# The second block's attention: projection weights split by quarters, one step after each piece of a projection

## The chip, the cores and the metric

The kernel runs on one core of a Trainium2 chip. The metric is device time in microseconds of one execution; the time quoted is the median of three runs. The profile is of one further execution.

## The reference, cut to what matters

Two transformer blocks are computed on 512 tokens of width 1024, in 32-bit floats. The first block mixes (short convolution and FFT), attends to a memory and runs a mixture of experts. The second block, where the change lies, has two kinds of attention heads, read from one projection `w_in_2`, then an output projection and a gated feed-forward part:

```
u = rms_norm(h, norm1_w)
proj = u @ w_in                               # 1024 x 3072
dq, dk, dv, sq, sk, sv = split(proj)
y_diff = two softmaxes per head, subtracted:  (softmax(q0 k0) - lam * softmax(q1 k1)) @ dv
y_sb   = stick-breaking:  sigmoid(z) * product over later keys of sigmoid(-z), @ sv
h = h + concat(rms_norm(y_diff), rms_norm(y_sb)) @ w_out
h = h + (silu(u2 @ w_gate) * (u2 @ w_up)) @ w_down
```

## The kernel before

**Weights.** Every weight matrix is read in chunks of 1024 rows by 256 columns (1 MB, held as 128 partitions by 8 row groups `k` by 256). A product is made with three matmuls in TensorE's rounded 32-bit format: upper part times upper part, upper times lower, lower times upper. So each chunk, once loaded as `raw`, is split into an upper part `wh` (ScalarE copies with rounding, line 241) and a lower part `wl` (VectorE subtracts `wh` from `raw`, line 259).

**The stream.** The chunks stand in a list `stream`, in order of use. `chunk(name)` is called at the head of each projection. It calls `split_to`, which splits the chunk that comes next: there are two buffers for `wh`, so one chunk is in use and one is prepared. `rest` makes the lower part, gives the raw buffer back, and calls `load_to`, which issues the next load from SyncE's queue (line 218). For the chunks of this part of the kernel `wh` is one instruction of 128x2048 and `wl` another. The set `calm` is empty in this kernel.

**The attention part.** The order of the units is `UNITS`: a stick-breaking pair of heads ("s", 0), two pairs of difference heads ("d", 0) and ("d", 1), and ("s", 1). A unit has three chunks, q, k and v, so there are twelve: sq0, sk0, sv0, dq0, dk0, dv0, dq1, dk1, dv1, sq1, sk1, sv1. A projection is made in four pieces, with a call of `tick` after each. In `proj_N` (all v chunks, and dq and dk) a piece is one tile of 128 tokens against all of the chunk, 24 matmuls in order of `k` (from line 274 to line 276); in `proj_T` (sq, sk) the first two pieces use `k` 0 to 3 and the last two `k` 4 to 7. After two pieces of `proj_N` the bank is read out: for v by ScalarE (line 283) and VectorE (line 284), for dq and dk by a sum of squares (lines 1663 to 1668), and a power on GpSimd (line 380).

**The side work.** The heads of a unit run as a `Chain` of steps while later projections are made. `tick` adds the piece's cost to a model time `now`, and runs up to two steps of each of two chains that are due by that model. Letters name the steps: P, Q, R the scores of the query blocks, T the transposes of the weights (line 1495, read out at lines 280 and 281), A the product with v (lines 1507 to 1509), N and C the head norm (1519, 1535). Difference heads have F (line 1717), which finishes the weights of the last block before T. The order of instructions on every engine is the order in which this program writes them down; nothing is reordered by a scheduler.

```
def tick(piece=2.56):
    now[0] += piece
    for g in side[:2]:
        for _ in range(2):
            if g.steps and g.ready():
                g.step()
```

Of the kernel before, what the change touches and what calls it, by code (L numbers as in the profile page):

```python
# [11 lines left out]
F32 = mybir.dt.float32  # L12
F32R = mybir.dt.float32r
# [3 lines left out]
AF = mybir.ActivationFunctionType  # L17
ALU = mybir.AluOpType
# [17 lines left out]
UNITS = (("s", 0), ("d", 0), ("d", 1), ("s", 1))  # L36
# [13 lines left out]
HALVED = 5  # L50
# [35 lines left out]
def block_kernel(ctx: ExitStack, tc: tile.TileContext, a: dict, out: bass.AP, start="mix", stop="tail"):  # L86
    nc = tc.nc
# [12 lines left out]
    def cols(w, c, n=256):  # L100
        return w.rearrange("(k p) f -> p k f", p=P)[:, :, c * n:(c + 1) * n]

    stream = []
# [2 lines left out]
    plan = {}  # L106
    wide = {}
    home = set()
    calm = set()
    pools = {}  # L110

    def add(name, ap, j=None):
        plan[name] = len(stream)
        wide[len(stream)] = j
        stream.append(ap)
# [26 lines left out]
    if "tail" in run:  # L142
        w2 = a["w_in_2"][0]
        for kind, u in UNITS:
            for n, base in zip("qkv", (6, 8, 10) if kind == "s" else (0, 2, 4)):
                add((kind + n, u), cols(w2, base + u))
        for c in range(4):
            if c > 1:
                home.add(len(stream))
            add(("o2", c), cols(a["w_out_2"][0], c))  # L150
        wd = a["w_down_2"][0].rearrange("(k p) f -> p k f", p=P)
        for part, fs in enumerate(FF):
            for c in fs:
                add(("fg", c), cols(a["w_gate_2"][0], c))
                add(("fu", c), cols(a["w_up_2"][0], c))
            k0, k1 = 2 * fs[0], 2 * fs[-1] + 2
            for half in range(2):
                for c, k in enumerate(range(k0, k1, 4)):
                    add(("fd", part, half, c), wd[:, k:min(k + 4, k1), half * 512:half * 512 + 512])

    raws, parts, lows = {}, {}, {}

    room = list(ROOM[0])
    state = {"load": 0, "split": 0, "use": 0, "held": None, "later": None, "last": None,
             "limit": plan[0, "gu", 0] + EARLY if "moe" in run else len(stream)}

    def buffer(b, shape, dt, name):
        pool = rawp if b in ROOM[0] else pools["raw" if b in ROOM[1] else "raw3"]
        return pool.tile(shape, dt, tag=f"w{b}", name=name)

    def hl_pool(i):
        if i in home:
            return "slots"
        return "hl" if wide[i] is not None and wide[i] % 4 >= 2 else None

    def oldest():

        return max(state["use"] - 1, 0) if state["held"] is None else state["held"]

    def pieces(r, two):  # L180
        n = r.shape[1] // 2 if two else r.shape[1]
        return [slice(q, q + n) for q in range(0, r.shape[1], n)]
# [4 lines left out]
    def find(i, low):  # L187


        for q in [q for q in lows if q < oldest()]:  # L190
            room.append(lows.pop(q))
        expert, running = wide[i] is not None, "hl" in pools
        may = room if expert else always(room)
        if low:
            if state["last"] in may:
                may = [state["last"]]
        else:
            if running and len(room) < 2 and len(lows) < 4:
                return None
            if expert and not running:  # L200
                may = [b for b in may if (b in ROOM[0]) == (wide[i] < 2)]
            if not (expert and running) and len(always(room)) < 2 and len(always(lows.values())) < 2:
                may = [b for b in may if b not in ROOM[0]]
        if not may:
            return None
        b = may[0]
        room.remove(b)
        return b

    def load_to(n, queue=nc.sync):  # L210
        while state["load"] < min(n, state["limit"], len(stream)):
            i = state["load"]
            b = find(i, False)
            if b is None:
                return
            r = buffer(b, list(stream[i].shape), F32, "raw")
            for t in pieces(r, i < HALVED):
                queue.dma_start(r[:, t], stream[i][:, t])
            raws[i] = b, r
            state["load"] += 1  # L220

    def split_to(n):
        while state["split"] < min(n, len(stream)):
            i = state["split"]
            key = hl_pool(i)
            busy = sum(hl_pool(q) == key for q in range(oldest(), i))
            if key and key not in pools or busy == 2:
                return
            if key == "slots" and state["use"] + 2 <= i:
                return  # L230
            load_to(i + 1)
            if state["later"] is None and i not in home:
                b = find(i, True)
                if b is None:
                    return
                lows[i] = b
            pool = pools[key] if key else hlp
            b, r = raws.pop(i)
            h = pool.tile(list(r.shape), F32R, tag="s" if key == "slots" else "hi", name="wh")
            for t in pieces(r, i < HALVED):  # L240
                nc.scalar.activation(h[:, t], r[:, t], AF.Copy)  # L241
            parts[i] = h, None
            state["split"] += 1
            if state["later"] is None:
                rest(i, b, r, h)
            else:
                state["later"].append((i, b, r, h))

    def rest(i, b, r, h):
        if i in home:  # L250
            l = pools["slots"].tile(list(r.shape), F32R, tag="s", name="wl")
        else:
            if i not in lows:
                lows[i] = find(i, True)
            l = buffer(lows[i], list(r.shape), F32R, "wl")
        parts[i] = h, l
        engine = nc.gpsimd if i in calm else nc.vector
        for t in pieces(r, i < HALVED or i in calm):
            engine.tensor_tensor(l[:, t], r[:, t], h[:, t].bitcast(F32), ALU.subtract)  # L259
        room.append(b)  # L260
        state["last"] = b
        load_to(len(stream))

    def chunk(name):
        i = plan[name]
        assert i == state["use"], (name, i, state)
        state["use"] += 1
        split_to(i + 4)
        return parts.pop(i)
# [237 lines left out]
    def mixing():  # L507
# [200 lines left out]
        for ct in range(4):  # L708
# [18 lines left out]
            out_half(ps0, ct, 0, *first)  # L727
        state["held"] = None
        split_to(state["use"] + 3)

        hT = []
# [217 lines left out]
    def moe():  # L949
# [20 lines left out]
        later = state["later"] = []  # L970
        state["held"] = state["use"]
        split_to(state["use"] + 4)
        state["held"] = state["later"] = None
        rest(*later.pop(0))

        wide_ = rp.tile([P, NT, NE + K], F32, name="logit")
# [88 lines left out]
        for args in later[:2]:  # L1065
            rest(*args)
# [323 lines left out]
    def tail():  # L1390
# [47 lines left out]
        class Chain:  # L1438
# [12 lines left out]
            def step(self):  # L1451
                name, work, cost, _ = self.steps.pop(0)
                work()
                now[0] += cost
                self.at[name] = now[0]
# [6 lines that stand above are left out]
                        g.step()  # L1462
                if not g.steps:
                    side.remove(g)

        def drain():
            while side:
                g = side[0]
                g.step()
                if not g.steps:  # L1470
                    side.pop(0)

        def parts2(name, late=None):

            r = proj_T(name, hT, late=late, tick=tick)
            return r, slot([P, 2, 2, S])
# [380 lines left out]
        for part, fs in enumerate(FF):  # L1857
            actT = []
            slots_ = []
            for c in fs:  # L1860
                g = []
                for ps in proj_T(("fg", c), h2T, late=(lambda: rsd.visit_to(4)) if c == 0 else None):
                    if rb is None:
                        rb = spread(rsd.rstd(EPS_2), NT, sc, "rbc")
                    t = sc.tile([P, S], F32, tag="om", name="fg", bufs=3)
# [4 lines left out]
                for j, ps in enumerate(proj_T(("fu", c), h2T)):  # L1870
# [3 lines left out]
                    q = len(actT) % 4  # L1874
# [3 lines left out]
            for half in range(2):  # L1878
                s = slice(half * 512, half * 512 + 512)
                ps = [bank() for _ in range(NT)]  # L1880
                for c in range((nf + 3) // 4):
                    h, l = chunk(("fd", part, half, c))
                    n = min(4, nf - 4 * c)
                    for i in range(NT):
                        t = slice(i * P, (i + 1) * P)
# [37 lines left out]
    if "tail" in run:  # L1923
        if "mix" not in run:
            with tc.tile_pool(name="tc", bufs=1) as tp:
                for _ in tail_constants(lambda shape: tp.tile(shape, F32, name="c%d" % len(shape) + str(shape[-1]))):
                    pass
        tail()
    else:
        dump()  # L1930
# [24 lines left out]
```

## Time and profile before

| | us |
|---|---|
| median of three runs | 2212.07 |
| lowest and highest run | 2211.58, 2212.27 |
| the profiled execution, its own time | 2213.85 |
| span of the profiled execution, first to last instruction | 2212.1 |

The profile's page gives busy time by engine, and TensorE's granted clock as a share of 2.4 GHz (0.50 is 1.2 GHz). The twelve attention projections and their side work run from about 1550 to 1764 us of the span; the rest of the second block follows. Times of rows below are us from the span's start.

### The profile page before, as it was taken

The numbers are of one execution on the slowest core, as the hardware profiler recorded it, in microseconds if no ns is written. First come the engines' busy times: TensorE is split into PE (matmuls) and PEld (weight loads), VectorE is DVE, ScalarE is ACT, GpSimd is POOL, SyncE is SP. The second block draws the span as 40 slices with busy tenths as digits, with TensorE's granted clock in tenths as the row PEclk, the third lists the DMA queues.
The fourth block names the chain that finished last, engine by engine and source line by source line (L and its number), as shares of the span: only waits on it lengthen the run. The fifth ranks groups of instructions, "written<-read, shape, count | busy, mean of one in ns | idle before, by whom it ended". The sixth has DMA issues, their size and how long they took to land. (4 is left out here: it accounts for less than half of the span.)

```text
span 2212.1 us, 28473 instructions
## 1 busy us (share of the span) xinstructions
PE 2155.5 (97%) x11282; PEld 1821.3 (82%) x11282; DVE 1594.7 (72%) x1630; ACT 1286.2 (58%) x1365; POOL 372.2 (17%) x237
## 2 busy tenths in 40 slices
PE   8999997999999999999999999998999889999999
PEld 7889897888888888888888888887888788888887
DVE  6555556999999999989898999987676754333342
ACT  5234445777777777777777777774654544221221
POOL 1220015212121212121212112110321000100110
PEclk9999998999999999999999999999999999999999
DMA  6422236999999999999999999997122112322222
GB/s 210 135 66 96 78 114 226 363 376 358 365 346 373 355 373 358 364 360 366 363 363 368 365 364 366 370 352 248 51 64 68 58 58 72 100 95 95 96 86 86
DMA packets 162095, 518.17 MB, mean 234 GB/s; under 512 B 14040, under 2 KB 82531, under 8 KB 129126
## 3 DMA queue, kind: packets, MB, share of 16 engines
q1 hardware_dynamic: 148886, 488.06, 59.7%
q0 software_dynamic: 13056, 28.24, 4.8%
q8 instruction: 90, 1.47, 0.3%
q14 instruction: 47, 0.39, 0.1%
q10 hardware_dynamic: 16, 0.00, 0.0%
HBM read 510.28 MB, written 22.13 MB: 241 GB/s over the span
## 5 line engine op out<-in xcount | busy, mean ns | idle before, releaser
L259 DVE TENSOR_TENSOR wl<-raw,wh 128x2048 fp32r<-128x2048 f32 (+1 forms) x468 | 1046.0, 2263 | 242.9 <-ACT wh L241 241.2
L241 ACT ACTIVATE wh<-raw 128x2048 fp32r<-128x2048 f32 (+1 forms) x468 | 870.8, 1892 | 219.1 <-PE b L1165 70.9
L1164 PE MATMUL b<-wh,xh 128*128 128x512 f32 x1024 | 412.2, 403 | 0.0
L1165 PE MATMUL b<-wh,xl 128*128 128x512 f32 x1024 | 401.8, 392 | 0.0
L274 PE MATMUL b<-wh,s 128*128 128x256 f32 (+2 forms) x904 | 281.3, 311 | 2.5 <-ACT s L280 2.5
L276 PE MATMUL b<-wh,s 128*128 128x256 f32 (+2 forms) x904 | 277.4, 307 | 1.0 <-DVE s L284 0.8
L1170 PE MATMUL b<-wl,xh 128*128 128x512 f32 x1024 | 277.6, 392 | 0.0
L275 PE MATMUL b<-wl,s 128*128 128x256 f32 (+2 forms) x904 | 277.1, 307 | 0.3 <-DVE wl L259 0.3
L1170 PEld LDWEIGHTS b<-wl,xh 128*128 128x128 f32 x1024 | 192.2, 188 | 43.6
L1164 PEld LDWEIGHTS b<-wh,xh 128*128 128x128 f32 x1024 | 192.9, 188 | 41.9 <-ACT xh L280 0.3
L1165 PEld LDWEIGHTS b<-wh,xl 128*128 128x128 f32 x1024 | 193.1, 189 | 39.5 <-DVE xl L281 0.4
L1212 PE MATMUL b<-wh,ah 128*128 128x512 f32 x508 | 200.3, 394 | 0.7 <-ACT ah L280 0.7
L1213 PE MATMUL b<-wh,al 128*128 128x512 f32 x508 | 199.4, 393 | 1.4 <-DVE al L281 1.4
L274 PEld LDWEIGHTS b<-wh,s 128*128 128x128 f32 x904 | 175.0, 194 | 11.6 <-ACT s L280 3.0
L276 PEld LDWEIGHTS b<-wh,s 128*128 128x128 f32 x904 | 174.8, 193 | 8.5 <-DVE s L284 1.0
L275 PEld LDWEIGHTS b<-wl,s 128*128 128x128 f32 x904 | 175.1, 194 | 7.3 <-DVE wl L259 0.5
L1278 POOL DMA_INDIRECT acc<-y,res x30 | 57.4, 1914 | 688.4 <-ACT y L1277 688.4
L1216 PE MATMUL b<-wl,ah 128*128 128x512 f32 x508 | 159.0, 394 | 0.0
L415 PE MATMUL b<-s,wh 128*128 128x512 f32 (+1 forms) x348 | 134.1, 388 | 1.5 <-ACT wh L241 1.5
L416 PE MATMUL b<-s,wh 128*128 128x512 f32 (+1 forms) x348 | 132.9, 384 | 0.0
L274 PE MATMUL b<-s,wh 128*128 128x512 f32 (+1 forms) x324 | 123.9, 383 | 1.0 <-ACT s L283 1.0
L275 PE MATMUL b<-s,wh 128*128 128x512 f32 (+1 forms) x324 | 123.5, 381 | 0.8 <-DVE s L284 0.8
(377 smaller groups left out, 2874.5 us busy)
## 6 DMA issues: line engine op xcount, KB each, us to landing
raw<-in_w_gate_up_dram SPq DMA_DIRECT2D x254, 1024.0 KB
raw<-in_w_down_dram SPq DMA_DIRECT2D x138, 1024.0 KB
raw<-in_w_in_dram SPq DMA_DIRECT2D x19, 1024.0 KB
raw<-in_w_gate_dram SPq DMA_DIRECT2D x11, 1024.0 KB
raw<-in_w_up_dram SPq DMA_DIRECT2D x11, 1024.0 KB
raw<-in_w_out_dram SPq DMA_DIRECT2D x8, 1024.0 KB
raw<-in_w_k_dram SPq DMA_DIRECT2D x8, 512.0 KB
raw<-in_w_q_dram SPq DMA_DIRECT2D x4, 1024.0 KB
```

Source lines behind the costliest of these rows:

```text
L241: nc.scalar.activation(h[:, t], r[:, t], AF.Copy)
L259: engine.tensor_tensor(l[:, t], r[:, t], h[:, t].bitcast(F32), ALU.subtract)
L274: nc.tensor.matmul(ps, ah, bh, start=(first and j == 0), stop=False)
L275: nc.tensor.matmul(ps, ah, bl, start=False, stop=False)
L276: nc.tensor.matmul(ps, al, bh, start=False, stop=(last and j == n - 1))
L415: nc.tensor.matmul(r[j][:, :n], ah, bh, start=q == 0, stop=False)
L1164: nc.tensor.matmul(ps[q], xh[:, k, :], wh[:, q, :], start=(k == 0), stop=False)
L1165: nc.tensor.matmul(ps[q], xl[:, k, :], wh[:, q, :], start=False, stop=False)
L1170: nc.tensor.matmul(ps[q], xh[:, k, :], wl[:, q, :], start=False, stop=(k == ND - 1))
L1212: nc.tensor.matmul(ps[s], ah[:, q, :], wh[:, kk, c], start=(q == 0), stop=False)
L1213: nc.tensor.matmul(ps[s], al[:, q, :], wh[:, kk, c], start=False, stop=False)
L1216: nc.tensor.matmul(ps[s], ah[:, q, :], wl[:, kk, c], start=False, stop=(q == ND - 1))
```

## The change

Nine of the twelve chunks, those of the units ("d", 0), ("d", 1) and ("s", 1), are put into `calm`. `split_to` no longer splits such a chunk at once. It hands it to a new function `drip`, which lays five steps into a list `waiting`. Steps 0 to 3 make one quarter of the upper part each (two row groups `k`, 128x512, ScalarE); steps 1 to 4 make one quarter of the lower part each, one quarter behind (VectorE). Step 4 also gives the raw buffer back and issues the next load. `tick` ends with one step out of `waiting`, behind the side work that it ran. `split_to` begins by running whatever is still waiting, so the fifth step stands at the head of the next projection, the one that uses this chunk. The old use of `calm` (halves on GpSimd), which no chunk had, is taken out.

```
+            if (kind, u) != UNITS[0]:
+                calm.add(len(stream))
             add((kind + n, u), cols(w2, base + u))
...
+    def dripped(n=0):
+        while len(waiting) > n:
+            waiting.pop(0)()
+
+    def drip(i, b, r, h):
+        low = []
+        def lower(t):
+            if not low:
+                low.append(buffer(lows[i], list(r.shape), F32R, "wl"))
+                parts[i] = h, low[0]
+            nc.vector.tensor_tensor(low[0][:, t], r[:, t], h[:, t].bitcast(F32), ALU.subtract)
+
+        def step(q):
+            m = r.shape[1] // 4
+            if q < 4:
+                t = slice(q * m, q * m + m)
+                nc.scalar.activation(h[:, t], r[:, t], AF.Copy)
+            if q > 0:
+                lower(slice(q * m - m, q * m))
+            if q == 4:
+                room.append(b)
+                state["last"] = b
+                load_to(len(stream))
+
+        waiting.extend(lambda q=q: step(q) for q in range(5))
+
     def split_to(n):
+        dripped()
         while state["split"] < min(n, len(stream)):
...
             h = pool.tile(list(r.shape), F32R, tag="s" if key == "slots" else "hi", name="wh")
+            if i in calm:
+                state["split"] += 1
+                drip(i, b, r, h)
+                continue
...
-        engine = nc.gpsimd if i in calm else nc.vector
-        for t in pieces(r, i < HALVED or i in calm):
-            engine.tensor_tensor(l[:, t], r[:, t], h[:, t].bitcast(F32), ALU.subtract)
+        for t in pieces(r, i < HALVED):
+            nc.vector.tensor_tensor(l[:, t], r[:, t], h[:, t].bitcast(F32), ALU.subtract)
...
                 if not g.steps:
                     side.remove(g)
+            dripped(max(len(waiting) - 1, 0))
```

## Rows read from the trace of the kernel before

**Rows 1.** The timeline of PE: start, length; in brackets the idle time and its releaser.

```profile
1624.70 0.87 PE L1686 MATMUL b<-ident,gn 128*128 128x128 f32 x6 [0.67 <-DVE gn L1676]
...
1664.07 1.75 PE L1495 MATMUL b<-ident,e 128*128 128x128 f32 x7 [7.52 <-DVE e L1717]
...
1733.51 0.50 PE L1507 MATMUL b<-ath,s 128*128 128x512 f32 x1 [1.98 <-DVE atl L281]
...
1766.38 0.65 PE L1535 MATMUL b<-ident,hr 128*128 128x128 f32 x4 [2.61 <-POOL hr L380]
```

**Rows 2.** Line 259 on DVE, 1570 to 1775: who on PE waited for it (us, times).

```profile
  PE b L275: 0.3, 1
```

**Rows 3.** The timelines of ACT and DVE: copy and subtraction of 128x512.

```profile
1578.55 0.63 ACT L1564 ACTIVATE s<-t 128x512 fp32r<-128x512 f32 x1 [1.36 <-DVE t L1563]
...
1579.21 0.69 DVE L1565 TENSOR_TENSOR s<-t,s 128x512 fp32r<-128x512 f32 x1 [0.70 <-ACT s L1564]
```

**Rows 4.** The timeline of PE: first matmul of dq0, dk0 (and its 24th), dv0, dq1, dk1, dv1.

```profile
1590.31 0.36 PE L274 MATMUL b<-wh,s 128*128 128x256 f32 x1
...
1607.11 0.36 PE L274 MATMUL b<-wh,s 128*128 128x256 f32 x1
...
1609.95 0.28 PE L276 MATMUL b<-wh,s 128*128 128x256 f32 x1
...
1625.33 0.36 PE L274 MATMUL b<-wh,s 128*128 128x256 f32 x1
...
1648.67 0.39 PE L274 MATMUL b<-wh,s 128*128 128x256 f32 x1
...
1677.55 0.36 PE L274 MATMUL b<-wh,s 128*128 128x256 f32 x1
...
1694.89 0.36 PE L274 MATMUL b<-wh,s 128*128 128x256 f32 x1
```

**Rows 5.** The timeline of DVE: last instructions written down ahead of each projection's head.

```profile
1597.51 0.48 DVE L284 SCALAR_TENSOR_TENSOR s<-b,rr,s 128x256 fp32r<-128x256 f32 x1 [0.55 <-ACT s L283]
...
1610.78 0.23 DVE L1668 TENSOR_SCALAR gr<-gr,rr 128x4 f32<-128x4 f32 x1
...
1629.04 1.40 DVE L284 SCALAR_TENSOR_TENSOR s<-b,gq,s 128x512 fp32r<-128x512 f32 x2
...
1656.77 0.48 DVE L284 SCALAR_TENSOR_TENSOR s<-b,rr,s 128x256 fp32r<-128x256 f32 x1 [0.54 <-ACT s L283]
1658.57 2.29 DVE L259 TENSOR_TENSOR wl<-raw,wh 128x2048 fp32r<-128x2048 f32 x1 [1.31 <-ACT wh L241]
...
1663.27 0.75 DVE L1717 SCALAR_TENSOR_TENSOR e<-e,dr 128x512 f32<-128x512 f32 x1
...
1679.81 0.23 DVE L1668 TENSOR_SCALAR gr<-gr,rr 128x4 f32<-128x4 f32 x1
...
1695.90 1.40 DVE L284 SCALAR_TENSOR_TENSOR s<-b,gq,s 128x512 fp32r<-128x512 f32 x2
```

**Rows 6.** The timelines of PE and ACT at the start: first chunk, split by halves.

```profile
10.61 0.58 PE L415 MATMUL b<-s,wh 128*128 128x256 f32 x1 [1.51 <-ACT wh L241]
...
9.51 1.05 ACT L241 ACTIVATE wh<-raw 128x1024 fp32r<-128x1024 f32 x1
```

**Rows 7.** Windows: stretch, its length, busy time (instructions) by engine, granted clock, DMA.

```profile
1590.30:1593.30 3.00, 3.00 (x27) 3.00 (x28) 2.79 (x5) 3.00 (x7) 0.00 (x0) 1.00 0.00 0
...
1602.00:1606.00 4.00, 4.00 (x32) 3.87 (x31) 3.76 (x12) 2.22 (x7) 1.67 (x1) 1.00 0.81 262
...
1664.00:1666.00 2.00, 1.93 (x9) 1.60 (x11) 1.53 (x12) 1.25 (x5) 0.00 (x0) 0.50 0.67 227
...
1734.00:1736.00 2.00, 2.00 (x9) 1.81 (x8) 1.86 (x9) 0.00 (x0) 0.00 (x0) 0.50 1.02 328
1736.00:1738.00 2.00, 2.00 (x12) 1.42 (x11) 1.13 (x6) 0.80 (x3) 0.00 (x0) 0.64 0.60 198
```

**Rows 8.** The timeline of DVE: a wait for PE between the splits.

```profile
1643.60 0.29 DVE L1746 CUSTOM_DVE_ANT_0 e<-b,bias 128x128 f32<-128x128 f32 x1 [2.15 <-PE b L276]
```

More of the change, by code (lines that the diff above doesn't have):

```diff
@@ L108, in block_kernel @@
     home = set()
-    calm = set()
+    calm, waiting = set(), []
     pools = {}
```

## The prediction, made before the changed kernel ran

> **What bounds the kernel now.** I read the page first, then the timeline of PE through the twelve attention projections, for its idle time, then those of ScalarE and VectorE around each projection's head. PE has work nearly all the time; what can be won is what its idle rows hold [rows 1]. The long one, 7.52 us at 1664.07, is T of unit ("d", 0) waiting for F, and in front of F on VectorE stands a split: the lower part of dk1 runs 1658.57 to 1660.86, F ends at 1664.02 [rows 5]. The 1.98 us at 1733.51 (A of the same kind, one unit later) are of the same sort. The 2.61 us at 1766.38 come from GpSimd's power, behind VectorE's work; the first chunk of the output projection, whose split stands before it, is not among the nine. On the other side, the split as it is hardly ever holds PE up: 0.3 us in all of this stretch [rows 2], because a chunk is ready one whole projection before its use. That lead is what the change spends.
>
> **The change part by part.** *Price of the pieces.* The whole lower part takes 2.29 us [rows 5]. A quarter is 128x512; the nearest rows of that form take 0.69 us on VectorE and 0.63 us on ScalarE [rows 3]. Four cost 2.76 us where one cost 2.29, so 0.5 us more per chunk, and a little more on ScalarE. Between neighbours on the same queue I take 0.6 us per lower quarter and 0.5 per upper one, since such instructions overlap a little. In busy time this is about 10 us over nine chunks on engines with gaps; it costs nothing by itself. The cost is in the order.
>
> *When the last quarter is there.* The step behind piece 4 of a projection writes upper quarter 4 and lower quarter 3 of the next chunk; lower quarter 4 is written down at the head of that chunk's own projection. Both stand on VectorE's queue behind everything that the earlier pieces left there: side work, and the reading out of the last bank. In `proj_N` a piece's 24 matmuls follow each other at 0.1235 us (1607.11 to 1609.95 for 23 steps, [rows 4]) in order of `k`, so the first piece needs lower quarter 4 at its 20th matmul, 2.35 us after its first. That a matmul waits only for the part it reads, and not for the whole tile, is seen at the start of the kernel: the first chunk is split by halves, the first upper half ends at 10.56 and PE starts at 10.61 [rows 6]. So PE stands still at a head if VectorE is later than PE's first matmul there by more than 2.35 us, less the added quarters. I go through the heads; "ends" are of the last VectorE instruction written down ahead of the head.
>
> dq0: PE starts at 1590.31 and needs quarter 4 at 1592.66 [rows 4]. VectorE ends at 1597.99 [rows 5], and is busy 2.79 of 3 us with the score scans while PE makes that piece [rows 7], so three added quarters lie on its way, 1.8 us, and the fourth after them: 1600.45. PE loses **7.8**.
>
> dk0: PE needs it at 1609.46 [rows 4]. VectorE ended at 1611.0 [rows 5], with a split ahead of the step T that now is gone, but T's read-out is then paced by PE and ScalarE; behind it come quarter 3 (0.6) and quarter 4 (0.6): 1612.25. PE loses **2.8**.
>
> dv0: VectorE ended at 1630.4 [rows 5], with waits for GpSimd in which two quarters hide. The first one delays the scaling before PE's transposes (PE already waited there, [rows 1]), so PE starts 0.6 later; quarter 4 is there at 1631.5, needed at 1625.33 + 0.6 + 2.35 = 1628.3. PE loses 0.6 + 3.2 = **3.8**.
>
> dq1: VectorE ends at 1657.25 [rows 5]; one quarter ahead of a head norm (0.6), upper quarter 4 ahead of ScalarE's read-out (0.5) and the last (0.6) give 1659.0, and PE needs it at 1651.0 [rows 4]: 8 us. But this is the stretch of the 7.52 us. PE now waits at the head, and F is done when PE comes to T (head's last matmuls 0.7, a norm and the scores 1.5, piece two 3.0, T's first transposes 0.4: 1664.6 against 1664.07). So the long wait is only moved, at **+0.5**; two small waits ahead of it, whose split is gone, give back **-0.6**.
>
> dk1: VectorE ends at 1680.0 [rows 5]; about 1.6 us of quarters and ScalarE's copies do not hide, and quarter 4 follows: 1682.3 against 1679.9. PE loses 2.4, less 0.5 that T waits there today: **1.9**.
>
> dv1: VectorE ends at 1697.3 [rows 5], with the added 1.2 us at 1698.5; needed at 1697.24. PE loses **1.3**.
>
> sq1 and sk1 start with 16 matmuls on the upper part of `k` 0 to 3 alone and need quarter 4 only in piece three: nothing. At sk1 the split goes from in front of A's weights, which takes 0.6 off the 1.98 us and the slow clock behind it; at sv1 the head loses some 3 us. Up to the 2.61 us at 1766.38 [rows 1], which VectorE and GpSimd pace, the two together come to **-0.2**.
>
> The sum of waits is 7.8 + 2.8 + 3.8 + 0.5 - 0.6 + 1.9 + 1.3 - 0.2 = 17.3 us. Losses at early heads are not made good later: VectorE itself waits for PE in between, 2.15 us at 1643.60 [rows 8], so PE's delay goes through to it.
>
> *The clock.* After the 7.52 us the granted clock is 0.50, the lower level of 1.2 GHz, and after the 1.98 us it is 0.50 in 1734 to 1736 and 0.64 in 1736 to 1738 [rows 7]: 1.0 + 0.7 = 1.7 us lost behind that one. I put 1.7 behind the long waits of dq0 and dv0, half of it behind dk0, dk1 and dv1, whose waits come in two parts of 1 to 1.5 us, nothing at dq1, which pays already; 6.0, of which about 1 falls into the waits themselves. That is 5 us.
>
> *Transfers.* Each next load is issued one projection later, when quarter 4 is done. The windows show a load of 1 MB in 1602 to 1606 at 262 GB/s [rows 7], so about 4 us, and its chunk is first touched after the next projection's first piece, at least 12 us later. It stays hidden behind that projection; without that cover each of nine would cost up to 4 us. SyncE's and GpSimd's queues get nothing else new. ScalarE's upper quarters are done before VectorE comes to them.
>
> *Sum.* 17.3 + 5 = 22.3 us on the profiled execution's 2213.85 gives 2236.1; that execution is 1.8 us above the median of the runs, so **2234** for the median, about 1.0% slower.
>
> *Bounds.* From below: added quarters cost nothing ahead of the last, no clock is lost, and sk1's wait goes fully (1.98 + 0.5 + 1.7) with sv1's head free: 6.0 + 0.1 + 3.4 - 1.1 + 0.5 + 0.7 - 4.2 = 5.4 us, 2217. From above: no quarter hides, each head a further 1 to 2 us, sv1's 2.5 us stay, and 1.7 us of clock at five heads: 28 + 8 = 36 us, 2248. Single prices between the ends go by the row that is nearest: full price where VectorE has no idle row, nothing where it waits for GpSimd or PE.
>
> **Rivals.** *Faster: the side work gets through.* Without upper and lower part ahead of it, F's chain starts at 1657.25 and not at 1660.86 [rows 5], so T waits 3.7 us less, and some 0.9 of slow clock goes; A's wait and its slow clock go (1.98 + 1.7), with 0.5 at the next T: 8.8 us, 2203. It decides if quarter 4 of dq0 is there by 1592.66. For it speak the two idle rows; against it the ends in [rows 5], all later than the need in [rows 4] even without one added quarter. The Trainium skill states the rule for it ("Perfetto Trace Analysis", section "Optimizing Scalar/DVE Operations"): where ScalarE and VectorE are not saturated but leave bubbles on other engines, breaking up instructions may let work finish sooner. By that rule alone the time would be 2203; the trace bears it out at T and A, not at the heads.
>
> *No change: PE's delay eats its later idle time.* If VectorE's chain to F at 1663 did not depend on PE, the early heads would only use up the 7.52 us, and the time would be about 2213. Against it: the wait at 1643.60 [rows 8].
>
> *Slower still: a matmul waits for the whole tile.* Then each head loses what it now overlaps, some 2 us in six places and more at sk1, 12 to 18 us on top: 2246 to 2252. Against it: [rows 6].
>
> **How the numbers follow.** The forecast has 0.80, faster 0.10, no change 0.06, the whole tile 0.04. About 0.2%, 4.4 us, is what a measurement of this kernel can tell from no change. Faster by more: 0.10. Within: 0.06 and the forecast's lowest edge, 0.07. Slower: 0.83. The range is the forecast's own bounds, 2217 to 2248; outside lie faster, no change and part of the last.
>
> **What would show it.** In the changed profile PE's longest waits should stand at line 275 or 274 in the first piece of dq0, dk0, dv0 and dq1, released by VectorE's `wl`, in sum over 20 us; T's 7.52 us should be gone from line 1495, with as much at dq1's head; the granted clock should fall to 0.50 behind dq0's head, where it is 1.00 now. If those waits are under 3 us in sum, the reading of VectorE's lag is wrong, and the first rival holds. If PE's lateness at 1764 is much under that at dv0's head, the second does. SyncE's loads should land long before their split.

## The result, and the profile after

The changed kernel takes 2240.4 us (median of four runs, 2236.69 to 2241.41) against 2212.12 for the kernel before (four runs; the 2212.07 above is of three): a ratio of 1.0122, with a 95% interval from 1.0109 to 1.0135. The execution profiled below took 2240.26 us, 26.4 more than the 2213.85 of the one before.

Lines have moved: 274, 275 and 276 of before are now 310, 311 and 312; the transposes T (1495) are 1532, F (1717) is 1754, A (1507) is 1544, and the head norm (1535) is 1572. The reading out of a bank (283, 284) is 319 and 320. New are 244, which makes a quarter of `wh`, and 238, a quarter of `wl`. In some of the experiments the lines stand one or two further down.

From the page of the changed kernel: span, busy time by engine, and the group of line 311.

```profile
span 2238.4 us, 28512 instructions
...
PE 2168.2 (97%) x11282; PEld 1830.9 (82%) x11282; DVE 1595.9 (71%) x1657; ACT 1289.2 (58%) x1392; POOL 368.9 (16%) x237
...
L311 PE MATMUL b<-wl,s 128*128 128x256 f32 (+2 forms) x904 | 282.4, 312 | 23.4 <-DVE wl L238 23.0
```

The last line holds the result in short: PE stood still for 23.0 us at this line because a quarter of `wl` was not yet there. On line 275 of before it was 0.3 [rows 2].

Where the time went is read in two steps. First, how long the stretch from sv0's first matmul to one fixed matmul of the output projection takes (windows, before and then after; the columns are those of [rows 7]):

```profile
1574.92:1840.04 265.12, 243.22 (x1829) 224.00 (x1828) 173.36 (x364) 138.96 (x293) 40.28 (x25) 0.95 0.20 64
```

```profile
1573.90:1866.40 292.50, 257.75 (x1829) 235.16 (x1828) 175.20 (x391) 142.12 (x320) 36.97 (x25) 0.91 0.19 58
```

27.4 us have been added here, so all of the loss lies in this stretch. The matmuls are the same, yet PE is busy 14.5 us longer (257.75 - 243.22), at a granted clock of 0.91 in the mean and not 0.95; it stands idle 12.9 us longer (34.75 against 21.90). VectorE and ScalarE, with 27 more instructions each, are busy only 1.8 and 3.2 us longer. The forecast's 10 us of busy time for smaller pieces came to 5.0, on engines with gaps; the loss is not there.

Second, the heads, that is, the starts of the projections. The first matmul of dq0, dk0, dv0, dq1, dk1 and dv1 in the timeline of PE after; each answers to a row of [rows 4]:

```profile
1589.32 0.36 PE L310 MATMUL b<-wh,s 128*128 128x256 f32 x1
...
1615.73 0.37 PE L310 MATMUL b<-wh,s 128*128 128x256 f32 x1
...
1640.37 0.36 PE L310 MATMUL b<-wh,s 128*128 128x256 f32 x1
...
1667.98 0.39 PE L310 MATMUL b<-wh,s 128*128 128x256 f32 x1
...
1696.59 0.36 PE L310 MATMUL b<-wh,s 128*128 128x256 f32 x1
...
1718.61 0.36 PE L310 MATMUL b<-wh,s 128*128 128x256 f32 x1
```

Minus the starts of before, PE is "late" by -1.0, +8.6, +15.0, +19.3, +19.0 and +23.7 us. (This execution entered the stretch 1.0 us early, so that dq0's -1.0 is zero.) What a head costs is the step to the next one: dq0 9.6, dk0 6.4, dv0 4.3, dq1 -0.3, dk1 4.7; dv1 1.4 more, and sq1, sk1 and sv1 together 1.3. The sum is 27.4.

PE's idle rows at the quarters, in the same timeline (those of dk1 and dv1, 0.40 to 1.14 us, left out), and one row ahead of dv0:

```profile
1592.96 0.39 PE L311 MATMUL b<-wl,s 128*128 128x256 f32 x1 [2.56 <-DVE wl L238]
...
1597.41 0.58 PE L311 MATMUL b<-wl,s 128*128 128x256 f32 x1 [3.01 <-DVE wl L238]
...
1599.43 0.58 PE L311 MATMUL b<-wl,s 128*128 128x256 f32 x1 [0.37 <-DVE wl L238]
...
1618.83 0.39 PE L311 MATMUL b<-wl,s 128*128 128x256 f32 x1 [1.29 <-DVE wl L238]
...
1621.01 0.58 PE L311 MATMUL b<-wl,s 128*128 128x256 f32 x1 [1.20 <-DVE wl L238]
...
1639.74 0.87 PE L1723 MATMUL b<-ident,gn 128*128 128x128 f32 x6 [1.27 <-DVE gn L1713]
...
1646.44 0.39 PE L311 MATMUL b<-wl,s 128*128 128x256 f32 x1 [3.41 <-DVE wl L238]
...
1674.21 0.58 PE L311 MATMUL b<-wl,s 128*128 128x256 f32 x1 [3.63 <-DVE wl L238]
...
1678.33 0.58 PE L311 MATMUL b<-wl,s 128*128 128x256 f32 x1 [2.06 <-DVE wl L238]
...
1774.33 0.58 PE L311 MATMUL b<-wl,s 128*128 128x256 f32 x1 [2.84 <-DVE wl L238]
```

The rows of line 311 stand in the first pieces of dq0, dk0, dv0, dq1 and, the last one, sv1; the row of 1723 is the transposes ahead of dv0. No row of T with 7.52 us is left, nor of A with 1.98 [rows 1]. The second column, the matmul's length, tells of the clock: 0.39 us at 1618.83, but 0.58 at 1621.01, where the granted clock is falling (windows under e9).

What stood in front of dq0's last quarter is seen in VectorE's timeline:

```profile
1592.22 0.68 DVE L238 TENSOR_TENSOR wl<-raw,wh 128x512 fp32r<-128x512 f32 x1
1592.82 1.22 DVE L1640 TENSOR_TENSOR_SCAN om<-om 128x512 f32<-128x512 f32 x1
1594.14 0.69 DVE L1641 TENSOR_TENSOR be<-be,om 128x511 f32<-128x511 f32 x1
1594.75 1.22 DVE L1640 TENSOR_TENSOR_SCAN om<-om 128x512 f32<-128x512 f32 x1
1596.07 0.69 DVE L1641 TENSOR_TENSOR be<-be,om 128x511 f32<-128x511 f32 x1
1596.68 0.68 DVE L238 TENSOR_TENSOR wl<-raw,wh 128x512 fp32r<-128x512 f32 x1
1597.28 0.48 DVE L320 SCALAR_TENSOR_TENSOR s<-b,rr,s 128x256 fp32r<-128x256 f32 x1
1598.30 0.48 DVE L320 SCALAR_TENSOR_TENSOR s<-b,rr,s 128x256 fp32r<-128x256 f32 x1 [0.54 <-ACT s L319]
1598.70 1.28 DVE L238 TENSOR_TENSOR wl<-raw,wh 128x512 fp32r<-128x512 f32 x2
```

The rows of line 238 at 1592.22 and 1596.68 and the first at 1598.70 are quarters two, three and four of dq0; they end where PE's three waits end. The second instruction at 1598.70 is the next chunk's. Between them stand the score scans of the side work (1640, 1641) and the reading out of the last bank (320). VectorE is never idle, except 0.54 us for ScalarE: the quarter is late because of its place in the queue. A quarter begins 0.60 us ahead of its neighbour (1596.68 to 1597.28), the price that the prediction took.

Windows of after behind that head show the slow clock, and the load that the fifth step issues (the last three columns are the granted clock, the DMA share and GB/s):

```profile
1600.00:1602.00 2.00, 2.00 (x12) 2.00 (x11) 0.00 (x0) 0.00 (x0) 0.00 (x0) 0.50 0.55 115
1602.00:1604.00 2.00, 2.00 (x13) 2.00 (x13) 0.00 (x0) 0.00 (x0) 0.00 (x0) 0.63 1.08 379
```

The load comes right behind the last quarter and is mostly over by 1604, 12 us ahead of dk0's first matmul. PE works through these 4 us without idle time, but loses 2 x (0.50 + 0.37) = 1.7 us of them to the clock, where it was at 1.00 before.

### The profile page after: what moved, and what is told of

It is laid out like the page before. It is cut to its first block, busy times and chain, and to the rows that moved or that the text cites. A ratio compares the mean times of both kernels' runs of the same rounds, so it can differ in the third digit from the quotient of the medians.

```text
span 2238.4 us, 28512 instructions
## 1 busy us (share of the span) xinstructions
PE 2168.2 (97%) x11282; PEld 1830.9 (82%) x11282; DVE 1595.9 (71%) x1657; ACT 1289.2 (58%) x1392; POOL 368.9 (16%) x237
## 5 line engine op out<-in xcount | busy, mean ns | idle before, releaser
L295 DVE TENSOR_TENSOR wl<-raw,wh 128x2048 fp32r<-128x2048 f32 (+1 forms) x459 | 1025.3, 2262 | 235.0 <-ACT wh L278 233.3
L278 ACT ACTIVATE wh<-raw 128x2048 fp32r<-128x2048 f32 (+1 forms) x459 | 853.4, 1891 | 218.3 <-PE b L1201 71.0
L311 PE MATMUL b<-wl,s 128*128 128x256 f32 (+2 forms) x904 | 282.4, 312 | 23.4 <-DVE wl L238 23.0
L310 PE MATMUL b<-wh,s 128*128 128x256 f32 (+2 forms) x904 | 284.5, 315 | 3.4 <-ACT s L316 2.6
L312 PE MATMUL b<-wh,s 128*128 128x256 f32 (+2 forms) x904 | 280.7, 311 | 1.0 <-DVE s L320 0.8
L310 PEld LDWEIGHTS b<-wh,s 128*128 128x128 f32 x904 | 178.0, 197 | 13.2 <-ACT s L316 3.1
L312 PEld LDWEIGHTS b<-wh,s 128*128 128x128 f32 x904 | 178.2, 197 | 8.4 <-DVE s L320 1.0
```

The lines of the kernel that those rows point to most:

```text
L295: nc.vector.tensor_tensor(l[:, t], r[:, t], h[:, t].bitcast(F32), ALU.subtract)
L310: nc.tensor.matmul(ps, ah, bh, start=(first and j == 0), stop=False)
L311: nc.tensor.matmul(ps, ah, bl, start=False, stop=False)
L312: nc.tensor.matmul(ps, al, bh, start=False, stop=(last and j == n - 1))
```

## The experiments

Each edit is against the changed kernel; "the stretch" is the one of the two windows above, and all medians are of runs beside the kernel before (2213.03, 2213.66, 2213.78 and 2213.15 in the four groups: e1 to e4, e5 to e8, e9 to e11, e12).

**e1: the five steps at once, at the head.** The pieces stay small, but stand where the whole split stood before.

```
                 drip(i, b, r, h)
+                dripped()
                 continue
```

> The same nine chunks and the same quarters, but all five steps of a chunk are written down at once at the head of the projection before, where the whole split stood. Theory (the last lower quarter stands too far back in VectorE's queue and PE waits for it at the head of its projection): the lead of one projection is back, so the waits at the heads go, the 7.52 us before T and the 1.98 us before A are back, and the time is that of the kernel before within 4 us, 2210 to 2216 us. Rival (the 27 added instructions on each of two engines cost it, wherever they stand): most of the 28 us stays, above 2230 us.

2211.89 us, ratio 0.9993 [0.9983, 1.0003]. The number of instructions costs nothing; the place does. In its profile the stretch is even 2.5 us shorter, though the interval of the ratio reaches 1. The row of T:

```profile
1664.19 1.76 PE L1533 MATMUL b<-ident,e 128*128 128x128 f32 x7 [6.45 <-DVE e L1755]
```

**e8: the same, with the next load issued one projection later,** as in the changed kernel.

```
-            if q > 0:
+            if 0 < q < 5:
                 lower(slice(q * m - m, q * m))
-            if q == 4:
+            if q == 5:
...
-        waiting.extend(lambda q=q: step(q) for q in range(5))
+        for q in range(5):
+            step(q)
+        waiting.append(lambda: step(5))
...
-            dripped(max(len(waiting) - 1, 0))
```

> The nine splits by quarters all at once at the head of the projection before, as in the run that did so, but the raw buffer goes back and the next load is issued one projection later, as in the changed kernel. Theory: the loads of 1 MB take about 4 us and still have more than 10 us, so nothing changes against that run: 2209 to 2215 us. Rival (the later loads are part of the loss): 2217 us or more.

2210.22, ratio 0.9986 [0.9977, 0.9995], and the lateness from head to head of e1 within 0.1 us. Later loads cost nothing.

**e3: only dq0's chunk in steps.**

```
-                if (kind, u) != UNITS[0]:
+                if (kind + n, u) == ("dq", 0):
```

> Only dq0's split is laid out by single steps as in the changed kernel; the other eight chunks are split whole as before. Theory (VectorE and ScalarE wait for PE between dq0's head and T, so PE's delay is not made good): what dq0's head loses, 9.9 us in the changed kernel's trace, comes through to the end, 2219 to 2224 us. Rival (the 7.52 us before T take it up): 2212 to 2216 us.

2221.47, ratio 1.0039 [1.0025, 1.0053]. Its head and its T:

```profile
1593.01 0.38 PE L311 MATMUL b<-wl,s 128*128 128x256 f32 x1 [2.57 <-DVE wl L238]
...
1597.47 0.58 PE L311 MATMUL b<-wl,s 128*128 128x256 f32 x1 [3.49 <-DVE wl L238]
...
1671.75 1.76 PE L1532 MATMUL b<-ident,e 128*128 128x128 f32 x7 [7.52 <-DVE e L1754]
```

8.6 us are lost at the head, and PE stays late by that much at the heads and at the end of the stretch, to within 0.2 us. T still waits 7.52, at 1671.75 and not at 1664.07: an early delay of PE does not use up a later wait.

**e7: only dq1's chunk in steps,** the head next to the 7.52 us (edit as in e3, with `("dq", 1)`).

> Only dq1's split is laid out by single steps; the other eight chunks are split whole as before, dk1's ahead of F among them. Theory: the 8 us that PE loses at dq1's head are the same 7.5 us that it lost before T, since both wait for the same work of VectorE; with dk1's split still ahead of F a wait before T stays as well: 2212 to 2217 us. Rival (the two waits add up): 2219 us or more.

2213.79, ratio 1.0004 [0.9995, 1.0013].

```profile
1650.02 0.39 PE L310 MATMUL b<-wh,s 128*128 128x256 f32 x1 [0.41 <-ACT wh L244]
1654.03 0.58 PE L311 MATMUL b<-wl,s 128*128 128x256 f32 x1 [3.63 <-DVE wl L238]
...
1658.16 0.58 PE L311 MATMUL b<-wl,s 128*128 128x256 f32 x1 [2.06 <-DVE wl L238]
```

6.1 us of waits at the head; T's long wait, of which a part was expected to stay, is gone, and PE comes to dk1 0.5 us earlier than before and to sq1 0.5 us later. The wait moved and was not added to.

**e9: only dk0's chunk in steps** (`("dk", 0)`).

> Only dk0's split is laid out by single steps; the other eight chunks are split whole. In the changed kernel's trace dk0's head is late by 2.6 us and then loses 2.8 us more to the slow clock, where the forecast had 2.8 and 0.85. Theory (a wait in two parts of 1.3 us costs as much slow clock as a long one): 2.5 to 3 us of lateness and 2 to 3 of clock come through to the end, 5 us more than the kernel before. Rival (the slow clock at dk0 was left over from dq0's waits in front of it): 3.5 us more, and the granted clock stays at 1.00 behind dk0's head.

2218.15, ratio 1.0019 [1.001, 1.0028]. Its two waits and a window behind them:

```profile
1608.67 0.39 PE L311 MATMUL b<-wl,s 128*128 128x256 f32 x1 [1.30 <-DVE wl L238]
...
1610.86 0.39 PE L311 MATMUL b<-wl,s 128*128 128x256 f32 x1 [1.21 <-DVE wl L238]
```

```profile
1612.00:1614.00 2.00, 2.00 (x16) 1.62 (x13) 1.76 (x2) 1.36 (x3) 0.30 (x1) 1.00 0.91 270
```

The head costs 3.0 us (2.5 of idle time, 0.5 of busy time), with the granted clock at 1.00 in every window around it. That is the profiled execution, which at 2215.39 us is the second fastest of eleven; they go up to 2220.10, and the median lies 4.4 us above the kernel before, between the theory's 5 and the rival's 3.5. So the 1.00 is shown for one execution. In the changed kernel the same two waits (1.29 and 1.20) were followed by this:

```profile
1620.00:1622.00 2.00, 0.99 (x4) 0.99 (x5) 0.95 (x3) 0.00 (x0) 1.56 (x1) 0.63 0.00 0
1622.00:1624.00 2.00, 2.00 (x12) 1.34 (x11) 0.00 (x0) 0.04 (x1) 0.45 (x1) 0.50 0.94 264
1624.00:1626.00 2.00, 2.00 (x7) 1.71 (x7) 1.32 (x2) 1.95 (x4) 0.00 (x0) 0.50 0.77 261
1626.00:1628.00 2.00, 2.00 (x13) 2.00 (x12) 1.62 (x3) 0.44 (x1) 0.00 (x0) 0.66 0.00 0
```

Against 1.00 PE's busy time in these four windows loses 0.99 x 0.37 + 2.00 x (0.50 + 0.50 + 0.34) = 3.0 us. With the 0.6 us more that the transposes ahead of dv0 wait (1.27 against 0.67), that is about the difference between 6.4 and 3.0. Windows from dk0's first matmul to dv0's, before and then after, give PE's busy time as 3.3 us longer:

```profile
1607.11:1625.33 18.22, 17.55 (x144) 16.27 (x142) 14.43 (x24) 10.56 (x20) 5.25 (x2) 1.00 0.18 58
```

```profile
1615.73:1640.37 24.64, 20.87 (x143) 18.74 (x142) 13.46 (x24) 11.45 (x24) 3.64 (x2) 0.86 0.14 43
```

**e12: dq0 and dk0 in steps,** to see whether the loss at dq0 makes the clock fall at dk0 (`in (("dq", 0), ("dk", 0))`).

> Only the chunks of dq0 and dk0 are split in steps; all else is as before. Alone, dq0 carried 7.7 us to the end and dk0 3.1, and at dk0 alone the granted clock stayed at 1.00 behind waits of 1.30 and 1.21. In the changed kernel, waits of 1.29 and 1.20 at the same place were followed by 0.50 and a cost of 6.4 at that head. Theory: the slow clock at dk0 in the changed kernel comes of what was lost before it on the same way (the long waits and the slow clock at dq0's head, 20 us earlier); then both waits stand here with a granted clock of 0.50 or 0.63 behind them, dk0 costs about 6, and the stretch is 14 us longer: some 0.6% over the kernel before, 2226 to 2229. Rival: the two heads are independent and the clock's answer to such waits is near an edge that differs by execution or by what is done at the following pieces; then the windows behind dk0's head stay at 1.00, dk0 costs 3, and the sum is 10 to 11 us: 2223 to 2225.

2226.46, ratio 1.0058 [1.0044, 1.0072]. The waits at dk0 in its timeline, and the window behind them:

```profile
1619.86 0.39 PE L311 MATMUL b<-wl,s 128*128 128x256 f32 x1 [1.30 <-DVE wl L238]
...
1622.04 0.39 PE L311 MATMUL b<-wl,s 128*128 128x256 f32 x1 [1.21 <-DVE wl L238]
```

```profile
1622.00:1624.00 2.00, 1.96 (x15) 1.54 (x16) 2.00 (x1) 0.18 (x1) 1.48 (x1) 1.00 0.33 65
```

The clock stays at 1.00 from 1616 to 1630, and dk0 costs 3.0 again, dq0 8.6: the losses add up to 11.6, as the rival said. The median came 1.5 us above the rival's band, at the lower edge of the theory's; the windows decide against the theory.

The same trace shows more at dq0. Up to dk0's head e12 has the same instructions as the changed kernel on PE, VectorE, ScalarE and GpSimd, and its first wait at dq0, 2.57 us, is the 2.56 there to within 0.01. Behind it stand, in the changed kernel and then in e12:

```profile
1593.56 0.42 PE L311 MATMUL b<-wl,s 128*128 128x256 f32 x1
```

```profile
1595.05 0.38 PE L311 MATMUL b<-wl,s 128*128 128x256 f32 x1 [2.57 <-DVE wl L238]
...
1595.51 0.28 PE L311 MATMUL b<-wl,s 128*128 128x256 f32 x1
```

The third matmul behind the one that waited takes 0.42 us in one and 0.28 in the other: the clock had fallen in one execution and not yet in the other. dq0 cost 9.6 us in the first and 8.6 in the second.

**e6: the fifth step with the fourth,** behind piece four, so that the last quarter stands ahead of the bank's reading out.

```
             dripped(max(len(waiting) - 1, 0))
+            if len(waiting) == 1:
+                dripped()
```

> As the changed kernel, but the fifth step runs right behind the fourth, after the fourth piece, and so ahead of the reading out of that piece's bank. Theory: VectorE's queue is the cause, and the read-out is a part of what stands in it: quarter 4 comes 1.5 to 3 us earlier at dq0, dk0, dv0, dk1, dv1 and sv1, and T comes 1.5 us earlier; 10 to 12 us less than the changed kernel, 2226 to 2232 us. Rival (only the side work ahead of it holds quarter 4 up): within 3 us of the changed kernel.

2226.94, ratio 1.0059 [1.0044, 1.0075]. About half of the loss goes: the waits at the heads of dv0, dv1 and sv1 are gone, dk0 keeps one of its two (1.29). The other half, above all dq0's 2.57 and 3.48, stays: there the side work stands in front.

**e4: the whole split behind the first piece.** Each chunk is split behind the side work of piece one, three pieces before its use.

```
-            dripped(max(len(waiting) - 1, 0))
+            dripped()
```

> As the changed kernel, but all five steps of a chunk run after the first piece of the projection before, behind the side work of that piece. Theory: every last quarter is there long before its head, dq0 too, since no side work is due after sv0's first piece; the split no longer stands ahead of F and of A's weights, so T's wait is 3 to 4 us shorter with its slow clock and A's 1.98 us go: 2202 to 2208 us, and 2 to 4 us less than with two steps after each piece. Rival (it is the spreading between side work that costs, not the lateness of the last quarter): within 4 us of the kernel before or slower.

2209.17, ratio 0.9984 [0.9974, 0.9993]: 1 us above what the theory allowed, and by its band the rival's (within 4 us of the kernel before, 3.9 here). This run can't tell the two apart, since its steps are no longer spread; e2 below does. The head waits are gone; T and what comes at sk1 are:

```profile
1658.14 1.76 PE L1532 MATMUL b<-ident,e 128*128 128x128 f32 x7 [3.90 <-DVE e L1754]
...
1725.48 0.69 PE L310 MATMUL b<-s 64*128 64x384 f32 x1 [2.14 <-DVE s L320]
```

T waits 3.6 us less. A's 1.98 has gone too, but a wait of 2.14 with two smaller ones has come ahead of it at sk1, where sk1's own split now stands among the side work.

**e2: two steps after each piece,** so that all five are done by piece three (`dripped(max(len(waiting) - 2, 0))`).

> As the changed kernel, but two steps after each piece, so that the fifth is written down after the third piece and not at the next head. Theory: the last lower quarter stands ahead of the fourth piece's side work and ahead of the reading out of the bank; only dq0's head still waits, about 2 us with 1 us of slow clock, and F no longer stands behind dk1's split, so T's wait is 3 to 4 us shorter and A's goes: 2203 to 2211 us. Rival (any spreading between the pieces costs, because the quarters hold up the side work): about half of the 28 us stays, 2222 to 2230 us.

2214.03, ratio 1.0005 [0.9996, 1.0015]: a miss for the theory, but far below the rival's 2222 to 2230. Steps that are spread, with the last one early, leave out most of the loss, so it is the lateness of the last quarter that brings it. T's wait fell to 4.13, but dq0's head kept one of 1.73, the transposes before dv0 one of 1.87, and sk1 the 2.14 of e4.

**e5: e4 for dk1 and sv1 alone** (`in (("dk", 1), ("sv", 1))`), the two chunks whose split stood in front of T and next to A.

> Only the two splits that stood ahead of a waiting step, dk1 (ahead of F and T) and sv1 (ahead of A's weights), are moved: all five steps run after the first piece of the projection before, behind its side work; the other seven chunks are split whole at the head as before. Theory: T's wait shrinks from 7.5 to about 3.9 us with its slow clock, as in the run with all nine moved so, sk1's new waits there (2.9 us) do not arise, and A's wait goes; part of the last is taken back at the head norm that GpSimd and VectorE pace: 2205 to 2209 us, the fastest so far. Rival (the gain of the nine is spread over all of them): between that run and the kernel before, 2209 to 2213 us.

2212.76, ratio 0.9996 [0.9987, 1.0005]: a miss, in the rival's band. T waits 3.90, but the gain is given back one piece later:

```profile
1684.32 1.18 PE L1532 MATMUL b<-ident,e 128*128 128x128 f32 x7 [2.34 <-DVE e L1754]
```

dv1's whole split, still at the head, now stands in front of the next F. PE came to dk1 3.1 us earlier than before and to dv1 0.4 us later.

**e10: e4 for dk1 and dv1 alone** (`in (("dk", 1), ("dv", 1))`): dv1's split is moved behind that F, and sv1's stays at the head.

> Only dk1's and dv1's splits are moved, all five steps behind the first piece's side work of the projection before. With dk1 and sv1 so moved, T's wait had shrunk from 7.52 to 3.90 us, but the next T had waited 2.34 us in place of 0.48, as dv1's whole split stood ahead of its F. Theory: with dv1's split behind that F too, the second wait does not arise and PE stays 4 to 5 us earlier through dv1; a part is taken back at the head norm near 1766 us: 3 to 5 us less than the kernel before. Rival (VectorE's work as a whole sets the time of the second T, whatever stands ahead of F): the wait arises all the same, within 2 us of the kernel before.

2209.49, ratio 0.9978 [0.9969, 0.9987]; T waits 3.92, the next T not at all. Two chunks are enough, so the gain is not spread over all nine, as e5's rival had it.

**e11: e4 for all but sk1.**

```
-                if (kind, u) != UNITS[0]:
+                if (kind, u) != UNITS[0] and (kind + n, u) != ("sk", 1):
...
-            dripped(max(len(waiting) - 1, 0))
+            dripped()
```

> All steps behind the first piece for eight of the nine chunks; sk1's split stays whole at the head, since in the run with all nine it led to waits of 0.33, 0.46 and 2.14 us after sk1's first piece that the kernel before does not have to that size (0.54). Theory: those 2.4 us and their slow clock go, A's wait stays away: 5 to 8 us less than the kernel before, the fastest. Rival (VectorE and GpSimd pace the head norm near 1766 us, so what is won at sk1 is waited away there): as the run with all nine, 3 to 5 us less.

2208.38, ratio 0.9973 [0.9962, 0.9984], the lowest median of all, 5.4 us under the kernel before; its interval overlaps those of e10 and e4. PE is 7.7 us earlier at sv1's head; 4.0 of it are given back in sv1, in part at these rows, which had no such wait before:

```profile
1746.74 0.50 PE L1544 MATMUL b<-ath,s 128*128 128x512 f32 x1 [1.22 <-DVE atl L317]
...
1753.45 1.05 PE L1556 MATMUL b<-ones,ysq 128*128 128x1 f32 x8 [0.71 <-ACT ysq L1802]
```

Behind them 1.5 us are won again, at the head norm that waited 2.61 us before [rows 1] and waits 1.13 here.

## Why the prediction was right, and where it was off

Forecast was 2234 from a sum of 22.3 us: waits of 17.3 and clock of 5. Measured are 2240.4, inside the range, and 27.4 us in the stretch. By its own steps:

**The pieces cost nothing by themselves, the order does.** Shown by e1, and by 32 of the 36 quarters standing in a kernel that is faster (e11).

**Lateness at the heads.** For dq0 the first matmul stands at 1589.32, so the 20th would need its quarter at 1591.67; it starts at 1599.43: 7.8 us late, the forecast's 7.8. PE did not lose it in one wait but in three, for quarters two, three and four, with matmuls at the slow clock between them. At dk0 it waits 1.29 + 1.20 and loses 3.0 where the clock holds (e9, e12), forecast 2.8. At dv0 the transposes ahead wait 1.27 against 0.67 [rows 1], the forecast 0.6 more, and the head 3.41 against 3.2. At dk1 and dv1 the waits sum to 1.9 and 1.1, forecast 2.4 and 1.3. In sum PE waits 23.0 us for quarters, where the prediction looked for over 20.

Two small waits ahead of dq1 are gone, which gives back 0.7, forecast 0.6.

**The moved wait.** From dq1's head to dk1's the wait was to grow by 0.5 and the clock to cost nothing, as the stretch "pays already". Together that came to -0.3, but by two misses that cancel: PE's idle time fell by 1.4 (7.52 to 6.14), and its busy time grew by 1.1. That the sum came out so near is luck. e7 shows the same pair alone, -1.4 and +1.5.

**sk1 and sv1** were put at -0.2 and came to +1.3, with sq1: A's wait went, a row of 2.84 at sv1 came, and of the 4.6 us lost there 2.7 are given back behind it. ScalarE's upper quarters were to be done before VectorE comes to them; three times they were not, and VectorE waited 3.6 us for them in all.

**The clock was the mis-sized term.** The forecast gave 1.7 us behind a long wait, 0.85 behind one in two parts and nothing at dq1, 5 in all. Windows from one head's first matmul to the next one's show PE's busy time longer, for the same matmuls, by 3.7 us at dq0, 3.3 at dk0, 1.5 at dv0, 1.1 at dq1, 3.2 at dk1, and 1.8 from dv1 on: the 14.5. Of dq0's, 1.9 lie between its three waits (7.8 less 5.9 of idle time) and are in the 7.8 already; of the last, 1.5 belong to sq1, sk1 and sv1 and are in their 1.3. That leaves 11.1 us, where the forecast had 5. The waits, put at 17.3, came to 16.1: 7.8 at dq0, 2.5 at dk0, 0.6 and 3.4 for dv0, 1.5 at dk1 (net of what T waits before) and 1.1 at dv1, less 1.4 at dq1 and 0.7 ahead of it, and 1.3 for sq1 to sv1. The long waits of dq0 and dv0 cost what was forecast behind them (1.8 and 1.5 for 1.7); dk0 and dk1 cost over three times the 0.85, dq1 was not free, and dv1 cost 0.3. So in this execution a wait in parts was not cheaper than a whole one; in those of e9 and e12 it cost no slow clock at all at dk0.

**The rivals.** "No change" falls with e3, and with PE's lateness of 29.1 us at 1764 of before, more than the 15.0 at dv0. "Whole tile" falls with PE's three separate waits at dq0. "Faster" was wrong for this order but right in its mechanism: take the split out of F's way and T waits 3.6 us less (e4, e10, e11), as [rows 5] give it (1660.86 - 1657.25; the prediction says 3.7). What decides is where the last quarter stands, here at the next head. The Trainium skill's rule ("Perfetto Trace Analysis", section "Optimizing Scalar/DVE Operations") is that breaking up instructions may let work finish sooner where ScalarE and VectorE are not saturated but leave bubbles on other engines. The trace agrees only in a small part: quarters at the old place cut T's wait from 7.52 to 6.45 us (e1, whose interval reaches the kernel before), and the same quarters spread out gave 2240.4. The gain of e4, e10 and e11 has its pieces together at a later place, and no run moved an unbroken split there, so it is not shown to come of the breaking.

**Transfers** stayed hidden (e8); no row waits for `raw`.

**What stays open** is what decides whether such waits are followed by the slower level. The loss at dq0 is not it (e12). At dq0 the changed kernel and e12 differ after the same instructions and the same first wait, so it can differ from one execution to the next; that dk0's difference is of this kind is likely, but not shown. With it stays open how much of the 11.1 us another execution would show: the four runs of the changed kernel take from 2236.69 us, at a mean granted clock of 0.984, to 2241.41, at 0.981; the profiled one has 0.980.

## What to carry to other kernels

Work spread over the queue of an engine that runs in order is paid by its last piece: find where its consumer first needs it, and count what stands ahead of it in that queue then. To let urgent work through, move the whole of the other behind it, not a tail past the next need (2208.4 against 2240.4 us here). After each wait that goes, look at the next one in line: in e5 all that T had won was given back one piece later, and in e4 1.6 us of 4.8 at the next heads.

## What the runs showed of the hardware

The slower clock cost PE as much as the waits did, net of the waits that went: 14.5 us of longer busy time against 12.9 of idle time, in a stretch with 23.0 us of new waits. Waits equal to within 0.01 us were followed by the slower level in one execution and not in others, once even behind the same instructions (0.42 against 0.28 us for the same matmul at dq0).
